# One short first load of 8 KB rows, or two of 4 KB rows on the same queue, in an adaptive max-pool

## The chip, the cores and the metric

The kernel runs on one core of a Trainium2 chip. The metric is the device time of one execution in microseconds (us). Before the change it is 334.88 us, the median of three runs (334.83 to 334.99). Engine names are those of the profile: DVE is VectorE, ACT is ScalarE, POOL is GpSimd, SP is SyncE; a "q" behind a name is the engine's instruction queue, on which it also issues DMAs.

## The reference

The input is `x` with 32 x 256 x 4096 float32 values (134.2 MB), the output 32 x 256 x 256 (8.4 MB). With an output size of 256 every window has 4096 / 256 = 16 values, and each output is the largest value of its window:

```
for i in range(output_size):
    start = int(i * length / output_size)
    end = int((i + 1) * length / output_size)
    result[:, :, i] = np.max(x[:, :, start:end], axis=-1)
```

Windows do not overlap and none crosses a row, so the work is one long list of windows of 16 neighbouring values, each reduced to its maximum.

## The kernel before, in words

The list of 2,097,152 windows is dealt to the 128 partitions of SBUF, 16,384 windows to each. It is cut into two groups. In each group a partition owns one contiguous stretch of the list, so one load takes one contiguous row of DRAM per partition: n windows make a row of 64 x n bytes.

Group a is the list `group_a` (L42): a short load of `FIRST` = 128 windows (8 KB rows, 1 MB in all), twelve loads of `CHUNK` = 1024 windows (64 KB rows, 8 MB in all) and one of 1020. Group b (L44) is two loads of 1024 windows and one of 900. The loads of group a are taken from the end of each partition's stretch backwards (`a -= n`, L82), those of group b forwards.

All loads go to one SBUF tile, `ring`, which has two halves of 1024 + 152 windows. The long loads take the halves in turn, and each second use of a half is shifted by `GAP` = 152 windows. The long load of a half is pooled in two reduces, one of 872 windows and one of 152 (L98 to L101, calling `pooled`, whose one instruction is L56). They are ordered so that the reduce of 872 windows frees the place of the next load to that half; the load can then be issued while the reduce of 152 windows still runs. The results go to the tile `kept`, from which they are stored at the end.

The short load (L87) goes to windows 1024 to 1151 of the first half, behind the first long load's place (0 to 1023) and inside the place of the third long load (152 to 1175). It is pooled by a reduce of its own, 128 windows, 2048 values on each partition.

All loads are issued by SyncE on one queue (q1), in program order: the short load at L87, then the long loads at L96. The framework adds the waits: a load waits for the reduces that read the bytes it overwrites. Each load and store signals its completion on one of eight semaphores, which are taken in turn. At the end ScalarE issues the store of the last 900 windows on its own queue (q10, L114); the two stores from `kept` (L117) are issued by SyncE behind the last load. L148 is the end of the program, where SyncE waits for all transfers.

Of the kernel before, what the change touches and what calls it, by code (L numbers as in the profile page):

```python
# [1 line left out]

# [4 lines left out]


@with_exitstack
def kernel(  # L10
    ctx: ExitStack,
    tc: tile.TileContext,
    x: bass.AP,
    output_size: bass.AP,
    out: bass.AP,
):

    nc = tc.nc
    P = nc.NUM_PARTITIONS
    fp32 = mybir.dt.float32

    B, C, L = x.shape
    O = int(output_size)  # L30
    assert L % O == 0, (L, O)
    W = L // O
    total = B * C * O // P
    assert B * C * O % P == 0

    CHUNK = 1024
    GAP = 152
    FIRST = 128
    LOADS_A, LOADS_B = 13, 2

    LESS = 4
    group_a = [FIRST] + [CHUNK] * (LOADS_A - 1) + [CHUNK - LESS]  # L42
    last = total - sum(group_a) - LOADS_B * CHUNK
    group_b = [CHUNK] * LOADS_B + [last]  # L44
    assert 0 < last and last * (W + 1) <= CHUNK * W

    pool = ctx.enter_context(tc.tile_pool(name="pool", bufs=1))
    ring = pool.tile([P, 2 * (CHUNK + GAP) * W], fp32, tag="ring", name="ring")
    kept = pool.tile([P, total - last], fp32, tag="kept", name="kept")

    xw = x.flatten_outer_dims().rearrange("r (o w) -> (r o) w", w=W)
    ow = out.flatten_outer_dims().rearrange("r o -> (r o)")

    def pooled(dst, at, n):

        nc.vector.reduce_max(  # L56
            out=dst,
            in_=ring[:, at * W : (at + n) * W].rearrange("p (n w) -> p n w", w=W),
            axis=mybir.AxisListType.X,
        )  # L60

    taken = 0

    def group(n):

        nonlocal taken
        span = slice(taken * P, (taken + n) * P)
        taken += n
        return (
            xw[span].rearrange("(p n) w -> p (n w)", p=P),  # L70
            ow[span].rearrange("(p n) -> p n", p=P),
        )

    stores = []
    n_loads = 0
    base = 0
    for g, loads in enumerate((group_a, group_b)):
        xg, og = group(sum(loads))
        a = sum(loads) if g == 0 else 0
        for n in loads:  # L80
            if g == 0:
                a -= n  # L82
            xn = xg[:, a * W : (a + n) * W]
            dst = kept[:, base + a : base + a + n] if n != last else None
            if n == FIRST:

                nc.sync.dma_start(  # L87
                    out=ring[:, CHUNK * W : (CHUNK + n) * W], in_=xn
                )
                pooled(dst, CHUNK, n)  # L90
            else:

                low = n_loads % 2 * (CHUNK + GAP)
                moved = n_loads // 2 % 2
                at = low + moved * GAP
                nc.sync.dma_start(out=ring[:, at * W : (at + n) * W], in_=xn)  # L96
                if n != last:
                    cut = CHUNK - GAP if moved else GAP  # L98
                    parts = [(0, cut), (cut, n)]
                    for u, v in parts if moved else parts[::-1]:  # L100
                        pooled(dst[:, u:v], at + u, v - u)  # L101
                else:
                    end = (at + CHUNK) * W
                    last_kept = ring[:, end - n : end]
                    pooled(last_kept, at, n)
                n_loads += 1
            if g:
                a += n
        full = a - last if g else sum(loads)
        stores.append((og[:, 0:full], kept[:, base : base + full]))  # L110
        base += full
    assert taken == total

    nc.scalar.dma_start(out=og[:, full : full + last], in_=last_kept)  # L114
    tc.no_sync_barrier()
    for dst, src in stores:
        nc.sync.dma_start(out=dst, in_=src)  # L117


# [1 line left out]
_INS = ['x', 'output_size']  # L121
_OUTS = [((32, 256, 256), 'float32')]

_NUMBERS = {'output_size': 256}


# [26 lines left out]
```

## Time and profile before

| what | before |
|---|---|
| median of three runs | 334.88 us (334.83 to 334.99) |
| span of the profiled execution, first to last instruction | 333.1 us |
| DVE busy | 276.5 us, 32 reduces |
| DMA queue q1, share of 16 engines | 98.8%, 142.15 MB |
| DMA queue q10, share of 16 engines | 0.3%, 0.46 MB |
| mean DMA rate over the span | 428 GB/s |
| short load, issue to landing | 4.7 us |
| long load of 64 KB rows, issue to landing (median) | 24.0 us |

The span is what the hardware profiler saw of one execution, from the first to the last instruction of the program; the device time of a run also has what lies around it. Of the profiled execution the profile gives the span alone, so its own time is taken as the median beside it. Times in the timeline are microseconds from the start of the span. A line of the timeline reads: start, duration, engine, line of the code, operation, output and input, shape, how often, and in brackets how long the engine was idle before it and what ended that. A share of a DMA queue is the time of its packets over the time of all 16 DMA engines; a packet is one row that one engine moves, or the small write with which an engine marks that its part of a transfer is done.

### The profile page before, as it was taken

To read this page: it belongs to the slowest core of one execution; us is meant where nothing else is said; L and a number is where in the kernel's file an instruction comes from. 1 tells how busy PE (TensorE), PEld (TensorE's weight loads), DVE (VectorE), ACT (ScalarE), POOL (GpSimd) and SP (SyncE) were. 2 spreads that over 40 slices of the span, in tenths; PEclk is the share of its full clock that TensorE was granted. 3 is DMA by queue.
4 is the path that set the end of the run, shared out by engine and by line. 5 is a ranking of instruction groups with operands and counts; after the bars stand their busy time and mean duration, and the time that the engine had idled before them with its cause. 6 is when DMAs were issued, how large, how long until landed. Compare 5 with 4: busy or idle time off the path is not lost.

```text
span 333.1 us, 113 instructions
## 1 busy us (share of the span) xinstructions
DVE 276.5 (83%) x32; POOL 0.2 (0%) x4
## 2 busy tenths in 40 slices
DVE  2009979797997979799797979979797998979993
POOL 0000000000000000000000000000000000000000
DMA  9898989899898989899898989899898989899996
GB/s 378 378 504 378 504 378 496 386 441 441 378 504 378 504 378 496 386 457 425 378 504 378 504 378 504 378 441 441 385 494 377 504 378 504 378 458 443 421 413 285
DMA packets 2880, 142.61 MB, mean 428 GB/s; under 512 B 320, under 2 KB 320, under 8 KB 448
## 3 DMA queue, kind: packets, MB, share of 16 engines
q1 hardware_dynamic: 2736, 142.15, 98.8%
q10 hardware_dynamic: 144, 0.46, 0.3%
HBM read 134.22 MB, written 8.39 MB: 428 GB/s over the span
## 4 chain that ended last, share of the span: by engine, by line
DMA 57%; DVE 36%; DVEq 5%; issue 0%; SPq 0%
DMA ring<-in_x_dram 57%; DVE kept L56 36%; DVEq L148 5%; SPq L87 0%
## 5 line engine op out<-in xcount | busy, mean ns | idle before, releaser
L56 DVE TENSOR_REDUCE kept<-ring 128x152 f32<-128x2432 f32 (+3 forms) x31 | 261.4, 8472 | 51.5 <-DMA ring<-in_x_dram 51.5
L56 DVE TENSOR_REDUCE ring<-ring 128x900 f32<-128x14400 f32 x1 | 15.1, 15144 | 0.0
L134 POOL MEMSET const-bfloat16-1.0<- 128x1 bf16 x1 | 0.1, 102 | 0.0
L134 POOL MEMSET const-uint8-127<- 128x1 uint8 x1 | 0.1, 102 | 0.0
L134 POOL MEMSET const-float32-0.0<- 128x1 f32 x1 | 0.1, 99 | 0.2 <-issue 0.2
L134 POOL MEMSET const-float32-1.0<- 128x1 f32 x1 | 0.1, 99 | 0.0
## 6 DMA issues: line engine op xcount, KB each, us to landing
ring<-in_x_dram SPq DMA_DIRECT2D x1, 8160.0 KB, 23.9
ring<-in_x_dram SPq DMA_DIRECT2D x1, 7200.0 KB, 21.6
out_dram<-kept SPq DMA_DIRECT2D x1, 6718.0 KB, 37.2
ring<-in_x_dram SPq DMA_DIRECT2D x1, 1024.0 KB, 4.7
out_dram<-kept SPq DMA_DIRECT2D x1, 1024.0 KB, 18.1
out_dram<-ring ACTq DMA_DIRECT2D x1, 450.0 KB, 4.2
ring<-in_x_dram SPq DMA_DIRECT2D x14, 24.0
```

Of the source, the lines that this page charges most:

```text
L56: nc.vector.reduce_max(out=dst, in_=ring[:, at * W : (at + n) * W].rearrange("p (n w) -> p n w", w=W), axis=mybir.AxisListType.X,)
L134: nc = _bacc.Bacc("TRN2", target_bir_lowering=False, num_devices=1)
L148: with _tile.TileContext(nc) as tc:
```

## The change

The short first load of 128 windows becomes two loads of 64 windows. Each has rows of 4 KB, 0.5 MB in all. They are issued one behind the other on SyncE's queue, go to neighbouring places of the ring (windows 1024 to 1087 and 1088 to 1151) and each is pooled by a reduce of its own. As group a is walked backwards, the first of the two takes the last 64 windows of each partition's stretch and the second the 64 windows before them. All later loads, their places, the reduces on them and the stores stay as they were.

```
-    FIRST = 128
+    FIRST, FIRSTS = 64, 2
...
-    group_a = [FIRST] + [CHUNK] * (LOADS_A - 1) + [CHUNK - LESS]
+    group_a = [FIRST] * FIRSTS + [CHUNK] * (LOADS_A - 1) + [CHUNK - LESS]
...
+    first_at = CHUNK
...
                 nc.sync.dma_start(
-                    out=ring[:, CHUNK * W : (CHUNK + n) * W], in_=xn
+                    out=ring[:, first_at * W : (first_at + n) * W], in_=xn
                 )
-                pooled(dst, CHUNK, n)
+                pooled(dst, first_at, n)
+                first_at += n
```

## The prediction

> **What bounds the kernel now.** I read the page's first lines and queue shares, then the timeline of the front, then the DMA view of one steady stretch, then the timeline of the end.
>
> ```profile
> span 333.1 us, 113 instructions
> DVE 276.5 (83%) x32; POOL 0.2 (0%) x4
> ...
> q1 hardware_dynamic: 2736, 142.15, 98.8%
> q10 hardware_dynamic: 144, 0.46, 0.3%
> ```
>
> The 16 DMA engines are busy for 99.1% of the span and VectorE for 83%: the transfers are the bound, and what is left of their time is the front and the tail. The chain of waits on the page gives 36% to VectorE, but only because a chain that arrives at a landing steps back to the issue, and the issue had waited for VectorE. Whether the queue ran dry at such an issue is seen in the DMA view, here from 44.0 to 63.4 us, one whole period:
>
> ```profile
> DMA packets 144, 8.39 MB, mean 432 GB/s; under 512 B 16, under 2 KB 16, under 8 KB 16
> ...
> q1 hardware_dynamic: 144, 8.39, 99.9%
> ```
>
> It did not: 99.9% busy, with 128 rows of 64 KB and 16 small writes (the 16 engines' completion marks). Now the front:
>
> ```profile
> 0.73 0.37 SPq L87 DMA_DIRECT2D ring<-in_x_dram  x1
> 1.15 0.90 SPq L96 DMA_DIRECT2D ring<-in_x_dram  x2
> 5.46 2.29 DVE L56 TENSOR_REDUCE kept<-ring 128x128 f32<-128x2048 f32 x1 [5.46 <-DMA ring<-in_x_dram]
> 24.78 17.28 DVE L56 TENSOR_REDUCE kept<-ring 128x872 f32<-128x13952 f32 x2 [17.04 <-DMA ring<-in_x_dram]
> 44.14 17.28 DVE L56 TENSOR_REDUCE kept<-ring 128x872 f32<-128x13952 f32 x2 [2.08 <-DMA ring<-in_x_dram]
> ```
>
> The short load lands at 5.46, the first long one at 24.78, the second at 44.14: 19.32 and 19.36 us apart. VectorE needs 17.28 per long load and idles about 2.1. Last, the end:
>
> ```profile
> 290.99 0.33 SPq L96 DMA_DIRECT2D ring<-in_x_dram  x1
> 291.37 21.91 SPq L117 DMA_DIRECT2D out_dram<-kept  x2
> 295.63 17.28 DVE L56 TENSOR_REDUCE kept<-ring 128x872 f32<-128x13952 f32 x2 [2.07 <-DMA ring<-in_x_dram]
> 312.82 15.14 DVE L56 TENSOR_REDUCE ring<-ring 128x900 f32<-128x14400 f32 x1
> 328.00 0.37 ACTq L114 DMA_DIRECT2D out_dram<-ring  x1
> ```
>
> The last long load lands at about 312.67 (a wait on VectorE's queue ends there), just ahead of the last reduce; the big stores keep the engines full until 331.0, and the small store on the other queue follows: its rows end at 331.7, it lands at 332.23. Everything at the end (the reduce that starts at 295.63, the stores behind the last load) hangs on when the loads land, and these on the one packed stream that began at 1.73 us. **So the front moves the end one for one**, in both directions.
>
> **The change part by part.** One row's price comes from the trace's packet records (start, duration and size of each row on an engine). Rows follow one another on an engine every 305.8 ns at 8192 bytes and every 2414 ns at 65,536 bytes: (2414 - 305.8) / 57,344 = 0.03676 ns a byte, and 305.8 - 8192 x 0.03676 = 4.6 ns a row. The 3600-byte rows of the last store come out as 137.0 by it and follow every 137.6: the line holds below 8 KB too, for stores.
>
> Removed: 8 rows of 8192 bytes on each engine, 8 x 305.8 = 2446 ns. Added: 16 rows of 4096 bytes, by the line 4.6 + 150.6 = 155.2 ns each, 2483 ns, and one more completion mark, which takes 6 ns from its start to the next row's. Sum: 2483 + 6 - 2446 = **+0.04 us** on the packed stream, and so at the end. A 4 KB load row is not in the trace. From both sides: no cheaper than the 3600-byte row (16 x 137.6 = 2202, -0.24 us), no dearer than the 8 KB row (16 x 305.8 = 4893, +2.45 us). I take the line's value, as 4096 is nearest to 3600 and that row is on the line.
>
> The Trainium skill (DMA: Bandwidth & Descriptors, section on the iDMA fabric) tells of a stream of 1 MiB loads with 4 KiB rows, issued from SP, at 408.7 GB/s. By that, an estimate from the page, 1 MiB takes 2.57 us, and the term would be +0.12 in place of +0.04; no run so far shows it.
>
> **SP.** One issue more. The short load's takes 0.37 us, the next start is 0.42 behind the first. So the second half is issued at about 1.15, the first long load at 1.57 instead of 1.15, the second at 2.05 instead of 1.62. Each is early enough: the short load's rows begin on the engines between 1.73 and 2.27, which is 1.00 to 1.55 after its issue; by that delay the second half's rows are ready at 2.15 to 2.70 and the first long load's at 2.57 to 3.12. The first half keeps the quickest engine until 1.74 + 0.41 (a first row, 317 ns late on average) + 7 x 0.155 = 3.24, the second half until 4.5. Cover 0.5 and 1.4 us. Cost nothing; without the cover, its lack.
>
> **The ramp.** The 16 first rows took 626 ns on average against 309, and all rows of the short load together cost each engine 0.42 us more than 8 x 309. If it is a wait for the first data, 4 KB rows pay the same: nothing. Bounds: gone (-0.42), or paid again by the second half (+0.42). I take nothing, because the first long load, behind the short one on the same queue, shows no such ramp: its first rows take 2418 (one 2442), as everywhere.
>
> **VectorE.** One reduce of 2048 elements (2285 ns) becomes two of 1024. The reduces of 2432 and 13,952 elements take 2676 and 14,686: 1.0425 ns an element and 141 ns; so 1.21 us each, 2.42 in all. They lie in the 17 us before 24.78, and nobody waits for them before the third long load, which overwrites their place and waits anyway for a reduce that ends at 39.5. That load may get one more wait on an event long past; its issue leads the queue's need by 4.6 us (39.50 against the landing at 44.13). Nothing.
>
> **The tail.** At the end SP runs a list of waits, each for two of eight completion events, and one event comes after the small store's (28 ns, 68 from its start to the next). One load more turns the eight round by one; the store's event may stand one wait earlier in the list: 0 or +0.07. I take 0.
>
> Sum: +0.04. The profiled execution spans 333.06 us; the median of the three runs, 334.88, is 1.8 above it, which I take to stay. 334.88 + 0.04 = 334.92, and with half of the tail's doubt 334.95 us. A measurement of this kernel tells about 0.2%, 0.67 us, from no change; this is far inside it.
>
> **The rivals.**
>
> *Each load pays a start of its own (slower).* From issue to landing the short load took 4.73 us, its rows at full pace need 2.45: 2.3 us are latency. If the engines ran dry between the halves and the stream began anew, that is +2.3, 337.2 us. It decides as soon as the second half's rows come over 0.5 us later than worked out above. For it: the halves are only 0.5 MB, 1.25 us of cover where a long load gives 19. Against: none of the 15 gaps between long loads shows it, nor the one between the short and the first long load. The dear 4 KB row (+2.45, 337.3) has nearly the same price; the line through three sizes speaks against it. Together 0.10.
>
> The Trainium skill (the same page, section on the anatomy of one DMA) gives about 2.0 us fixed per transfer, and its rules want 1 MiB or more per DMA, so halves of 0.5 MB go against it. An estimate by it is 336.9 if that were paid in line. The landings 19.32 us apart, where eight rows of 2414 make 19.31, disagree for queued loads.
>
> *The ramp is paid again.* +0.42 and the +0.04: 335.35. Chance 0.08.
>
> *The ramp shrinks.* Shorter rows get the engines going sooner: up to -0.42, 334.5. For it: the ramp is the only loss ahead of the tail; against: the waits there look like latency, which does not know the row's length. Chance 0.08. To be faster by over 0.67 us, the whole ramp and another 0.3 us (of the 1.00 from issue to first row, say) would have to go: 0.03.
>
> *The change does not do what it says*, and the halves wait for each other. The long load beside the short one was issued at once, into the next bytes of the same ring, so disjoint parts are kept apart. This would look like the first rival and is counted there.
>
> **How the numbers follow.** Forecast (no more than 0.2 us off) 0.71, ramp again 0.08, ramp smaller 0.08, dear halves 0.10, much faster 0.03. Within 0.2%: 0.71 + 0.08 + 0.08 = 0.87; slower 0.10; faster 0.03. The range takes in both ends of the ramp and the lower end of the row's price, 334.5 to 335.5; outside lie 0.13, the row's upper end (337.3) among them, which goes with its rival.
>
> **What would show it.** Right: rows of 4096 bytes about 155 ns apart; the second half's first row directly behind the first half's mark; the first long load landing at 24.8, at most 0.1 later; two reduces of 1.21 us; every later landing shifted by the same few hundredths; 20 marks for 16 engines become 21, queue q1 with 144 packets more. Wrong: an idle gap on the engines between 3.2 and 4.5 us, or rows of 4096 bytes at 200 ns or more, with all landings late by as much.

## The result, and the profile after

The changed kernel takes 335.23 us (median of 21 runs, 335.00 to 336.12), the kernel before on the same chip 334.98 (21 runs, 334.81 to 335.23). The ratio is 1.0013 with a 95% interval of 1.0007 to 1.0018, that is 0.23 to 0.60 us more. This is within 0.2%, as forecast, and in the range, but the +0.04 of the forecast's sum was too small. The runs have an upper tail that those of before do not have in this set: 15 of 21 lie from 335.00 to 335.43, the other six from 335.58 up to 336.12, four of them from 335.94 on.

The profiled execution is one of that tail, 335.98 us. The page of the changed kernel, the lines that answer to those of before:

```profile
span 334.2 us, 116 instructions
DVE 276.6 (83%) x33; POOL 0.2 (0%) x4
...
q1 hardware_dynamic: 2880, 142.15, 98.6%
q10 hardware_dynamic: 144, 0.46, 0.3%
```

Queue q1 has the 144 packets more, and no more bytes. Its share fell by 0.2 points, which is idle time of the DMA engines. The timeline of the front (start, duration, engine, line, operation; in brackets the idle time before and what ended it) shows where the delay arises:

```profile
0.73 0.86 SPq L88 DMA_DIRECT2D ring<-in_x_dram  x2
1.64 39.32 SPq L98 DMA_DIRECT2D ring<-in_x_dram  x3
4.44 2.44 DVE L56 TENSOR_REDUCE kept<-ring 128x64 f32<-128x1024 f32 x2 [4.44 <-DMA ring<-in_x_dram]
25.92 17.28 DVE L56 TENSOR_REDUCE kept<-ring 128x872 f32<-128x13952 f32 x2 [19.04 <-DMA ring<-in_x_dram]
45.28 14.69 DVE L56 TENSOR_REDUCE kept<-ring 128x872 f32<-128x13952 f32 x1 [2.08 <-DMA ring<-in_x_dram]
```

The first long load lands at 25.92 instead of 24.78, and from there to the second it is 19.36 us as before: all is lost ahead of 25.92. The end follows:

```profile
313.93 15.14 DVE L56 TENSOR_REDUCE ring<-ring 128x900 f32<-128x14400 f32 x1
329.11 0.37 ACTq L116 DMA_DIRECT2D out_dram<-ring  x1
```

Both lines are 1.11 us later than before; 1.14 us at the front came out as 1.11 at the end. The trace's packet records name the culprit. Fifteen engines go from the completion mark of the second half straight to their first 64 KB row (4.74 to 5.30 us; 4.59 to 5.09 before). One engine writes that mark at 4.73, has nothing until 5.29, and then takes 3378 ns for its first 64 KB row instead of 2418: it flows only from 6.25 us on. It does not catch up in the rest of the execution, which fits every engine having eight rows of its own in each load: the ends of the 16 engines' last rows of a load are 1.30 us apart in the first long load and still 1.19 in the last (0.52 and 0.44 before).

### The profile page after: what moved, and what is told of

Its sections match the earlier page's. It is cut to its first block, busy times and chain, and to the rows that moved or that the text cites. A ratio compares the mean times of both kernels' runs of the same rounds, so it can differ in the third digit from the quotient of the medians.

```text
span 334.2 us, 116 instructions
## 1 busy us (share of the span) xinstructions
DVE 276.6 (83%) x33; POOL 0.2 (0%) x4
## 4 chain that ended last, share of the span: by engine, by line
DMA 57%; DVE 36%; DVEq 5%; SPq 0%; issue 0%
DMA ring<-in_x_dram 57%; DVE kept L56 36%; DVEq L150 5%; SPq L88 0%
```

## The experiments

**My theory after the result:** the rows of the first long load come late to an engine, since it is now the third load in line on SyncE's queue. **The rivals:** short rows cost more at the front; a further DMA costs something wherever it stands; the late engine is chance. All kernels do the whole work, and each is compared with the kernel before on its own chip. The 95% intervals reach about 0.3 us to either side. Of the differences below 1 us, only those of the first set, long_first_2x4k, long_first_4x2k, two_queues_4x2k and late_long_a have an interval that leaves out no change; the other small ones are indications.

| kernel | median us (highest) | before | difference |
|---|---|---|---|
| changed, first set | 335.23 (336.12) | 334.98 | +0.25 |
| again | 335.22 (335.58) | 335.10 | +0.12 |
| one_dma_4k | 335.29 (335.36) | 335.10 | +0.19 |
| two_dma_8k | 337.44 (337.62) | 335.10 | +2.34 |
| four_dma_2k | 337.00 (337.54) | 335.10 | +1.90 |
| one_dma_2k | 335.30 (335.43) | 335.07 | +0.23 |
| long_first_8k | 335.33 (335.78) | 335.07 | +0.26 |
| long_first_2x4k | 335.47 (335.70) | 335.07 | +0.40 |
| long_first_4x2k | 335.73 (336.32) | 335.07 | +0.66 |
| two_queues_2x4k | 335.02 (335.26) | 334.96 | +0.06 |
| two_queues_4x2k | 335.37 (335.59) | 334.96 | +0.41 |
| late_long_a | 335.38 (335.58) | 334.96 | +0.42 |
| late_long_b | 339.79 (340.33) | 334.96 | +4.83 |

### The changed kernel once more

> The changed kernel once more, for a second trace. Its first trace had one engine that stood still for 0.55 us before its first 64 KB row and then took 3378 ns for that row instead of 2418, so that the first long load landed 1.13 us late. If that is chance, which falls on some executions, this trace shows another engine or none, the median stays 0.2 to 0.4 us above the kernel before, and single runs lie up to 1.1 above it. If it belongs to the change, the trace shows the same late engine and the first long load lands at 25.9 again.

+0.12 us; ratio 1.0005 (0.9997 to 1.0014). The difference is less than the 0.2 to 0.4 us that were expected. Two of 11 runs lie above 335.5, none as high as the 336 of the first set. The timeline of this second trace:

```profile
1.62 0.90 SPq L98 DMA_DIRECT2D ring<-in_x_dram  x2
4.51 2.46 DVE L56 TENSOR_REDUCE kept<-ring 128x64 f32<-128x1024 f32 x2 [4.51 <-DMA ring<-in_x_dram]
25.11 14.69 DVE L56 TENSOR_REDUCE kept<-ring 128x872 f32<-128x13952 f32 x1 [18.14 <-DMA ring<-in_x_dram]
```

No engine stands still between the halves and the long load, and each takes 2418 ns for its first 64 KB row: nobody waits for the long load here. It still lands at 25.11, 0.33 us later than before. So the late engine comes in some executions only, and there is a smaller loss without it.

### Short rows without a second DMA

```
+                h = n // 2
                 nc.sync.dma_start(
-                    out=ring[:, CHUNK * W : (CHUNK + n) * W], in_=xn
+                    out=ring[:, CHUNK * W : (CHUNK + GAP) * W].rearrange(
+                        "p (k f) -> p k f", k=2
+                    )[:, :, 0 : h * W],
+                    in_=xn.rearrange("p (k f) -> p k f", k=2),
                 )
-                pooled(dst, CHUNK, n)
+                pooled(dst[:, 0:h], CHUNK, h)
+                pooled(dst[:, h:n], CHUNK + GAP // 2, h)
```

> One load at the front as before the change, but its 128 windows go to two places of the ring with a gap between, so that each partition's 8 KB are written as two rows of 4 KB: 16 rows an engine, one DMA, one completion mark, no second issue. Two reduces after the one landing. Theory of the row size (short rows in the ramp give the engines more chances to be late): like the changed kernel, +0.2 to +0.4 us. Theory of the extra DMA (the second issue and the long load issued 0.49 us later): like the kernel before, +0.04 at most by the price of a row.

+0.19 us, ratio 1.0003 (0.9994 to 1.0012), all 11 runs within 0.3 us of one another. This is as much as the changed kernel lost, so by itself it fits the theory of the rows. The same with four pieces, rows of 2 KB (compared with the kernel of two pieces; the reduces follow suit), speaks against it:

```
-                h = n // 2
+                h = n // 4
...
-                        "p (k f) -> p k f", k=2
+                        "p (k f) -> p k f", k=4
...
```

> One load at the front, its 128 windows written to four places of the ring, so 32 rows of 2 KB an engine from one DMA with one mark: the rows of four_dma_2k without its three more DMAs and without its late long load. Theory of the rows (short rows at the front leave the engines waiting): like four_dma_2k, +1.5 us or more over the kernel before. Theory of the DMAs (several issues one behind the other, or the long load that comes late): the rows' own price alone, +0.1 to +0.35 us, and no idle engine between 3.5 and 6.5 us.

+0.23 us, ratio 1.0006 (0.9997 to 1.0015).

```profile
0.73 0.44 SPq L88 DMA_DIRECT2D ring<-in_x_dram  x1
...
25.30 17.28 DVE L56 TENSOR_REDUCE kept<-ring 128x872 f32<-128x13952 f32 x2 [16.88 <-DMA ring<-in_x_dram]
```

32 rows an engine cost hardly more than 16, and nothing like the 1.90 of four_dma_2k (below), which has the same rows. For that loss the theory of the rows falls; for the tenths of the change these two kernels do not decide it. What both have in common is a form of load that SyncE takes 0.44 us to issue instead of 0.37, and a longer ramp; the part of it that is neither price nor tail, 0.1 to 0.15 us, is not explained.

### Two DMAs without short rows

```
-                nc.sync.dma_start(
-                    out=ring[:, CHUNK * W : (CHUNK + n) * W], in_=xn
-                )
+                for q in (slice(0, P // 2), slice(P // 2, P)):
+                    nc.sync.dma_start(
+                        out=ring[q, CHUNK * W : (CHUNK + n) * W], in_=xn[q]
+                    )
```

> Two loads at the front, but cut by partitions (0 to 63, 64 to 127), each with 8 KB rows: 4 and 4 rows of 8 KB an engine, one mark and one issue more, one reduce. Theory of the extra DMA: like the changed kernel, +0.2 to +0.4 us and single runs near +1. Theory of the row size: like the kernel before, within 0.1 us.

+2.34 us, ratio 1.0070 (1.0057 to 1.0082), far beyond either theory. The timeline:

```profile
0.72 1.18 SPq L88 DMA_DIRECT2D ring<-in_x_dram  x2
...
8.00 2.29 DVE L56 TENSOR_REDUCE kept<-ring 128x128 f32<-128x2048 f32 x1 [8.00 <-DMA ring<-in_x_dram]
27.20 17.28 DVE L56 TENSOR_REDUCE kept<-ring 128x872 f32<-128x13952 f32 x2 [16.92 <-DMA ring<-in_x_dram]
```

The short data lands at 8.00 instead of 5.46. The records show why, and it is not the number of DMAs: from 4 us on nearly every 8 KB row takes 540 to 640 ns instead of 309, on all engines. Why the rows are slow is open, and so this cut tells nothing of the change, only of itself.

### The dose doubled

```
-    FIRST, FIRSTS = 64, 2
+    FIRST, FIRSTS = 32, 4
```

> Four loads of 32 windows with 2 KB rows: the dose of the change doubled again, 32 rows an engine and three issues more than before. By the price of a row alone, 32 x (4.6 + 75.3) + 3 x 6 against 2446 ns: +0.13 us, and up to 0.07 in the tail. If the loss comes with the rows or the DMAs at the front, it grows with them: +0.5 us or more, and the spread of its runs too. The long load is issued at about 2.6 us then; should its rows come to an engine that has run dry, the trace shows idle time between the last mark of the short loads and the first 64 KB row on most engines.

+1.90 us, ratio 1.0053 (1.0040 to 1.0065).

```profile
0.73 1.80 SPq L88 DMA_DIRECT2D ring<-in_x_dram  x4
2.57 39.34 SPq L98 DMA_DIRECT2D ring<-in_x_dram  x3
3.71 1.32 DVE L56 TENSOR_REDUCE kept<-ring 128x32 f32<-128x512 f32 x2 [3.71 <-DMA ring<-in_x_dram]
6.14 0.69 DVE L56 TENSOR_REDUCE kept<-ring 128x32 f32<-128x512 f32 x1 [1.11 <-DMA ring<-in_x_dram]
7.38 0.69 DVE L56 TENSOR_REDUCE kept<-ring 128x32 f32<-128x512 f32 x1 [0.56 <-DMA ring<-in_x_dram]
26.87 17.28 DVE L56 TENSOR_REDUCE kept<-ring 128x872 f32<-128x13952 f32 x2 [18.80 <-DMA ring<-in_x_dram]
```

The first two loads land about as quickly as their rows allow; the third lands at 6.14 and the fourth at 7.38, where 0.25 MB need 0.64 us. In the records most engines now have what one engine had in the change: between 3.5 and 6.5 us they stand still for half a microsecond and more or hold one row for 0.3 to 1.5 us too long, on short rows and on the first 64 KB row alike. Until 3.5 us they had lost no more than in the kernel before.

### The same loads, in full flow

```
-    group_a = [FIRST] * FIRSTS + [CHUNK] * (LOADS_A - 1) + [CHUNK - LESS]
+    group_a = [CHUNK] + [FIRST] * FIRSTS + [CHUNK] * (LOADS_A - 2) + [CHUNK - LESS]
...
-    first_at = CHUNK
+    first_at = 2 * CHUNK + GAP
```

with `FIRST, FIRSTS` of 128, 1, then 64, 2, then 32, 4.

> The kernel before with the order turned round: the first long load is issued first and the one short load of 8 KB rows second, into the free end of the other half of the ring. Control for the next two. The ramp is then paid by 64 KB rows: if it is a wait for the first data, within 0.2 us of the kernel before; if it goes by the row, up to 0.3 us faster.

> The two 4 KB loads of the change behind the first long load, when the engines are in full flow and both have been waiting on the queue for 19 us. Theory that the loss belongs to the front (cold engines, rows or DMAs that come just in time): against long_first_8k only the rows' price, +0.04 us, up to 0.11 with the tail. Theory that 4 KB rows or a second DMA cost so much anywhere: +0.2 to +0.4 us as in the change.

> The four 2 KB loads behind the first long load. Front theory: against long_first_8k only the price of the rows, +0.13 us (32 rows of 80 ns and three marks), up to 0.2 with the tail, where the same four loads at the front cost 1.9. Theory that short rows or the number of DMAs cost it anywhere: +1.5 us or more.

The control is 0.26 us slower than the kernel before (1.0008, 0.9999 to 1.0017): the ramp is no shorter with 64 KB rows, in its trace even 0.3 us longer an engine, so it does not shrink with longer rows. Against the control, two 4 KB loads cost +0.14 and four 2 KB loads +0.40. By the price of the rows and the tail (0.07 for one load more and 0.15 for three, below) 0.11 and 0.28 were due. Where four_dma_2k lost 1.90, the same four loads with 19 us of cover lose 0.40. **Of these 1.90 us most goes with the place at the front, not with the DMAs nor the rows.** For the two loads of the change the place shows no such difference: +0.14 in full flow, +0.12 and +0.25 at the front.

### The same loads, issued from two queues

```
+                odd = (first_at - CHUNK) // n % 2
-                nc.sync.dma_start(
+                (nc.scalar if odd else nc.sync).dma_start(
                     out=ring[:, first_at * W : (first_at + n) * W], in_=xn
                 )
```

> The change, but its second 4 KB load is issued by ScalarE on its own queue, beside the first. The long load is then issued at about 1.16 us as before the change, not at 1.64. Theory of the late long load: no execution 0.5 us or more above the median, and +0.04 to +0.25 us over the kernel before (price of the rows and a ramp as in one_dma_4k). Theory of the number of DMAs: as the change, with a late engine in one run of four.

+0.06 us, ratio 1.0001 (0.9992 to 1.0010), the highest of 11 runs at 335.26.

```profile
0.73 0.41 ACTq L89 DMA_DIRECT2D ring<-in_x_dram  x1
0.73 0.37 SPq L89 DMA_DIRECT2D ring<-in_x_dram  x1
1.15 0.90 SPq L99 DMA_DIRECT2D ring<-in_x_dram  x2
...
24.80 14.69 DVE L56 TENSOR_REDUCE kept<-ring 128x872 f32<-128x13952 f32 x1 [17.16 <-DMA ring<-in_x_dram]
```

The two halves go out side by side, the long load at 1.15 as before the change, and it lands at 24.80 (24.78 before). The rows and the number of DMAs are those of the change; what is gone is the line of issues. The difference to the change, 0.06 to 0.19 us, is within the intervals.

> four_dma_2k with its four short loads issued in turn by SyncE and ScalarE: the same rows, DMAs and marks, but the long load goes out at about 1.6 us instead of 2.57, and no short load waits for more than one issue ahead of it on its engine. Theory of late issues: most of the 1.9 us goes, +0.2 to +0.6 remains. Theory of the number of DMAs at the front: +1.5 us or more stays.

+0.41 us, ratio 1.0012 (1.0003 to 1.0021), 0.28 of it due by price and tail.

```profile
1.63 0.90 SPq L99 DMA_DIRECT2D ring<-in_x_dram  x2
...
25.21 14.69 DVE L56 TENSOR_REDUCE kept<-ring 128x872 f32<-128x13952 f32 x1 [18.26 <-DMA ring<-in_x_dram]
```

With the long load issued at 1.63 it lands at 25.21, not 26.87: of the 1.90 us of four_dma_2k 1.49 have gone. A second queue changes two things at once, the time of each issue and the number of lists from which the engines take rows; these runs do not separate them.

The Trainium skill (DMA: Bandwidth & Descriptors, section "Issuing engines are not separate DMA queues") says that issuing from several engines only saves the sequencer's issue time, which is usually small against the transfer. Here the long load goes out 0.49 us earlier with two short loads and 0.94 with four, and with four the kernel gains 1.49 us, more than the issue time that is saved; these short loads last only 0.64 us each.

### A late long load and nothing else

```
+    nc.vector.memset(kept[:, 0 : W * W], 0.0)
...
+                for _ in range(5):
+                    nc.vector.reduce_max(
+                        out=ring[:, 0:W],
+                        in_=kept[:, 0 : W * W].rearrange("p (n w) -> p n w", w=W),
+                        axis=mybir.AxisListType.X,
+                    )
                 pooled(dst, CHUNK, n)
```

> The kernel before, one short load of 8 KB rows, with one thing added: the first long load waits for five small VectorE reduces (256 values each on each partition, on zeroes, into the place that the load overwrites), so that it is issued at about 2.6 us instead of 1.15, as late as in four_dma_2k. No short rows, no further DMA. By the delay from issue to first row that the prediction took (1.00 to 1.55 us) the rows are ready at 3.6 to 4.2, the engines need them from 4.59 on: no loss, within 0.1 us of the kernel before. Theory that the late long load is what costs in four_dma_2k: +0.5 to +1.5 us and idle engines ahead of the first 64 KB rows.

+0.42 us, ratio 1.0014 (1.0004 to 1.0023). The delay came out larger than planned:

```profile
1.16 2.24 DVE L93 TENSOR_REDUCE ring<-kept 128x16 f32<-128x256 f32 x5
3.42 0.81 SPq L104 DMA_DIRECT2D ring<-in_x_dram  x2
5.52 2.29 DVE L58 TENSOR_REDUCE kept<-ring 128x128 f32<-128x2048 f32 x1 [2.13 <-DMA ring<-in_x_dram]
25.44 14.69 DVE L58 TENSOR_REDUCE kept<-ring 128x872 f32<-128x13952 f32 x1 [17.63 <-DMA ring<-in_x_dram]
```

Issued at 3.42, 2.27 us later than before, the long load costs 0.43 us an engine in the records: its first rows hold their engines up to 1058 ns too long. Taking 2418 ns back from each row's end, they flow from 5.05 to 5.78 us on, 1.6 to 2.4 us after the issue. By the prediction's delay the rows would have been ready at 4.42 to 4.97, with the engines free from 4.61 on; all sixteen were held. With no line ahead, then, the delay is 1.6 to 2.4 us and not 1.00 to 1.55.

> The same with nine small reduces: the first long load is issued at about 3.9 us. By the delay of 1.00 to 1.55 us the rows are ready at 4.9 to 5.5, some 0.35 us after the engines need them: +0.3 to +0.5 us. If rows in flow need longer from their issue than the first ones (2.5 us or more), +1.5 us or more. If even this costs nothing, the time of the issue is not what the change lost.

```
-                for _ in range(5):
+                for _ in range(9):
```

+4.83 us, ratio 1.0143 (1.0129 to 1.0157), with nine reduces in place of five. The framework put another long load ahead of the one that was to be late, so the queue never ran dry (that load was issued at 1.15, a landing follows at 24.92, 0.14 later than before), and it also turned round the last two loads, so that the work after the last landing is another one. It tells nothing of the delay, but it is a control for late_long_a: with nine of the small reduces at the front and a long load issued early, the engines take 2418 to 2425 ns for their first 64 KB row. The reduces themselves do not hold the rows up.

```profile
1.15 38.81 SPq L104 DMA_DIRECT2D ring<-in_x_dram  x3
1.15 4.05 DVE L93 TENSOR_REDUCE ring<-kept 128x16 f32<-128x256 f32 x9
...
24.92 17.28 DVE L58 TENSOR_REDUCE kept<-ring 128x872 f32<-128x13952 f32 x2 [17.03 <-DMA ring<-in_x_dram]
```

## Why the prediction was right, and where not

**One for one: right.** 1.14 us at the front of the profiled execution, 1.11 at the last reduce and store.

**The rows: right.** 4 KB rows follow one another every 155.3 ns; 155.2 was worked out. This is 16 x 4096 / 155.3 = 422 GB/s, more than the 408.7 that the Trainium skill states (DMA: Bandwidth & Descriptors, section on the iDMA fabric), whose +0.12 did not come. The halves follow without a gap, 6 ns from mark to row: the first rival, a start of its own for each load, did not occur between them. The 2.0 us fixed per transfer that the prediction sets beside this rival stand in the Trainium skill (DMA: Bandwidth & Descriptors, section on the anatomy of one DMA) for DMAs that GpSimd issues; the loads here come from SyncE, and did not pay it in line. VectorE's two reduces took 1.22 us each, against 1.21 worked out.

**The tail: the wrong one of two values.** I took 0 for "0 or +0.07". SyncE's waits at the end are paired from eight events, and the last store's event stands one wait earlier now: from the end of that wait to the end of the span it is 0.83 us before and 0.90 in both traces of the change and in every other kernel with 21 DMAs. With 23 DMAs the time from the last row to the end grows by 0.15.

**SyncE: the step that failed, in some executions.** "Each is early enough: [...] Cost nothing; without the cover, its lack." The issues stood where I put them within 0.07 us (1.16, 1.64, 2.11). One slip in the cover decides nothing: a first row of 155 ns that comes 317 ns late takes 0.47 us, not 0.41. In the second trace the step held, as nobody waited for the long load. But the delay of 1.00 to 1.55 us was that of the first row's record on idle engines, not of its flow. In long_first_8k, where the long load is the first of all, its rows flow, worked out as for late_long_a, 1.7 to 2.3 us after the issue, and up to 2.6 in the two other kernels of that kind. And the delay does not hold in a line: the late engine of the change flowed 4.6 us after the long load's issue, two that had stood waiting for it in four_dma_2k 4.0 us after, against 2.4 at most in late_long_a, where the load was late but alone. For one engine of the first trace the cover of 1.4 us was therefore none.

**The ramp: between the forecast and its rival.** The short loads' rows cost an engine 0.42 us beyond their pace before; in the two traces of the change 0.51 and 0.48. That is less than 0.1 us more, but it counts only from each engine's first row on. In the second trace five engines begin that row at 2.44 to 2.56 us, where none was later than 2.27 before; on average the first rows begin at 2.08 instead of 1.92. The ramp cost 0.1 us more in the first trace and 0.2 in the second, where it is most of the 0.33 by which the long load lands late. I had taken nothing, the rival +0.42. Why the starts were late is open.

The sum after the fact is 0.04 + 0.07 for rows and tail and 0.1 to 0.2 for the ramp, together 0.2 to 0.3, against medians of +0.25 and +0.12; on top comes up to 0.9 us in the highest runs. That the sum of +0.04 still gave a time so near is in part luck: the ramp and the tail were each put at nothing, and both are small.

What is shown: a long load that is issued late costs by itself (late_long_a), and most of the loss of four short loads goes when they are issued from two queues (1.90 to 0.41). That the late engine of the change is the same event is argued. For it: runs above 335.5 were 8 of 32 in the change and none of 11 in two_queues_2x4k, which at a rate of 8 in 32 would happen in (24/32)^11 = 4 cases of 100. Against: the bound of 335.5 was chosen afterwards, and the kernel before was 0.02 to 0.14 us faster beside two_queues_2x4k than beside the change; such runs occur elsewhere too, three of 11 in long_first_8k and one of 33 of the kernel before beside it (335.69); and only one trace shows the engine. A late issue alone does not give it: by those 2.4 us a long load issued at 1.64 flows by 4.04, and the first engine asked for it at 4.74. Open stays why a line makes the delay longer than the issues themselves, and why one engine alone is hit.

## What to carry to other kernels

Where DMA engines are the bound, what is lost at the front reaches the end nearly undiminished (1.14 us became 1.11), and the slowest of the engines counts. Behind several short first transfers, the price of their rows can matter less than how long before its turn the next transfer is issued: allow 2.4 to 2.6 us, more if others are in line ahead, or try to issue from two queues. One DMA more can also move the last event in the list of final waits; that was 0.07 us here, and as the events are taken in turn it can be counted out beforehand.

## What the runs showed of the hardware that was not expected

- Two loads of 64 partitions moved most of their 8 KB rows in 540 to 640 ns each, where one of 128 partitions takes 309, and landed 2.5 us later than the one that they replaced.
- An engine that falls behind at 5 us is behind at 313 us by nearly as much (1.30 and 1.19 us between the engines).
- The price of a row in flow is a line from 2 KB to 64 KB: 80 ns at 2 KB (79.9 by the line), 155.3 at 4 KB, 305.8 at 8 KB, 2414 at 64 KB.
